# Attention in a two-layer hybrid trunk: probabilities times values as full-width rounded products instead of 64-column fp32 tiles

## The chip, the core and the metric

The kernel runs on one core of a Trainium2 chip. The metric is the device time of one execution in microseconds (us); lower is better. TensorE (PE) does the matrix products and the transposes and writes them to PSUM; VectorE (DVE) and ScalarE (ACT) take them from there; GpSimd (POOL) has a few small powers; SyncE (SP) issues the DMAs.

## The reference, cut to what matters

A backbone of two layers works on 256 latent tokens and 256 context tokens of width 1024. Each layer mixes tokens by four parallel branches, A (a convolution module), B (windowed attention), C (retention) and D (global attention), merges them by gates, and ends with a feed-forward part. Layer 0 carries both kinds of tokens, layer 1 only the latent ones as queries (its keys and values still come from all 512). B and D have 8 query heads and 2 key heads of 64 columns. The place of the change is the last line of

```python
def attend(q, k, v, mask, sink):
    s = jnp.einsum('bhgqd,bhkd->bhgqk', q, k).astype(jnp.float32) * (HEAD_DIM ** -0.5)
    ...
    p = jax.nn.softmax(s, axis=-1)
    ...
    return jnp.einsum('bhgqk,bhkd->bhgqd', p.astype(v.dtype), v)
```

## The kernel before

All large products are done as three products of rounded operands (type fp32r): rounded part times rounded part, and each rounded part times the other's remainder. Weights come by DMA in pieces of 128x1024 (raw), are rounded on ScalarE (wh) and have their remainder taken on VectorE (wl), two halves of 512 columns each. Transposes and some small products are plain fp32.

The order of instructions on every engine is written by a planner within the program. `Model` keeps an estimated clock for each engine, `Engine.us` books each instruction's cost, and `Flow` places side work between the products of the main stream. The main stream (layer, `tm_group`, `proj_a`, `proj_c`, `merge`, `project`, the feed-forward part) issues three products at a time (`mm3`) and then calls `flow.poll()`. Side work stands in generators, which yield what their next step reads; a poll advances those whose data are there by the planner's clocks, in a fixed priority, with at most so many generators of a stream at a time and only while VectorE and ScalarE are not too far ahead of TensorE:

```python
    STREAMS = (("chain2", 3.0, 1), ("pv", 3.0, 1), ("main", 1.5, 2), ("aux", 1.5, 1), ("fill", 0.3, 1))
```

(name, limit in us, generators at a time; each stream is gone over twice in a poll.) The weights' splitting stands ahead of these streams with a limit of 3.0. `flow.until` and `flow.drain` poll without main products until something is done. A wait in the planner's time only orders the instructions; on the chip each engine runs its instructions in that order as soon as their operands are there.

Attention of one branch: `k_gen` and `q_gen` (stream aux) prepare keys and queries; `score_gen` (stream main) makes scores of two heads for one query tile, their exponentials and the normalised probabilities P; when both query tiles of a head pair c are there, it adds a `pv_gen` to stream pv. A `pv_gen` goes over its key blocks kc, four for latent queries (s = 0) and two for context queries (s = 1): four transposes of P into a PSUM bank (ptp), a copy to SBUF (PT), and two products with the values, one head each, that fill the upper and the lower 64 partitions of the bank pv:

```python
                pe.matmul(
                    pv[64 * i:64 * i + 64, 0:256],
                    st["kv"][kt // 2][:, 256 * (kt % 2) + off:256 * (kt % 2) + off + 64],
                    PT[kc][:, 256 * i:256 * i + 256], start=(kc == 0), stop=(kc == nk - 1),
                )
```

Each such fp32 product leaves two records in the trace, so one key block leaves four. At the end pv is rounded (yh) and its remainder taken (yl), which are operands of the merge products mb. There are eight `pv_gen` per branch in layer 0 and four in layer 1. A `score_gen` begins only while fewer than two generators stand in stream pv.

Order of the stages in layer 0: keys and queries of B, branch A's projections and D's queries (tm) with B's attention beside them; then `flow.drain("aux", "main", "pv")`; `merge(stB)` with D's attention beside it; the same drain again; `merge(stD)`; projections of C; `merge(stA)`; `merge(stC)`. Layer 1: A's projections, keys, queries and C's projections with B's attention; `merge(stB)`, whose first product mb waits until B is done, with D's attention beside it; `merge(stD)`, whose first mb waits until D is done; then C and A. The convolution of branch A (tiles co, zp) is on VectorE in the stream fill, the last in priority; it is needed before `merge(stA)`.

Of the kernel before, what the change touches and what calls it, by code (L numbers as in the profile page):

```python
# [21 lines left out]
# columns of the packed per-feature vectors (one layer)  # L22
V_NORM, V_ADAB, V_ADW, V_ADB, V_ALG, V_ALB, V_FDW, V_FDB, V_END = 0, 32, 80, 204, 208, 212, 216, 348, 392
# columns of the packed rows (one layer)
# [3 lines left out]
# groups of adaLN columns: worked out during the last merge, and in the gaps after the two projections  # L28
IN_MERGE = ((4, 5, 6, 7, 8, 9), (7, 8, 9))
IDLE = (((10, 11), (4, 5, 6)), ((10, 11), ()))  # L30
NT = 60      # [128, 512] work tiles
NRAW = 5     # weight pieces on the way in
SIDE = 8     # banks in use when the side work may take one more
NW = 5       # weight pieces as rounded part and remainder


class Model:
    """Estimated clocks of the engines: orders the instructions, decides nothing else."""
# [52 lines left out]
class Engine:  # L91
    """Passes instructions on and books them with the model."""
# [4 lines left out]
    def us(self, op, out, ins, kw):  # L97
        n = _size(out)
        if self.n == "PE":
            if op == "transpose":  # L100
                return 0.123
            if ins[0].dtype == F32R:
                return max(n, 256) / 2400 + 0.002
            if _size(ins[0]) <= 64:
                return 0.25
            return max(4 * n / 2400, 0.235)
        if self.n == "DMA":
            return max(0.1, 1.43e-3 * n)
        n = max([n] + [_size(x) for x in ins])
        psum = any(x.space == bass.MemoryType.PSUM for x in [out, *ins])  # L110
        if self.n == "ACT":
            aps = sum(1 for k in ("scale", "bias") if k in kw and hasattr(kw[k], "shape"))
            return n * 0.833e-3 + (0.05 if psum else 0.093) + 0.093 * aps + (0.06 if "accum_out" in kw else 0)
        if self.n == "POOL":
            return 0.1 + 0.14 * n
        if op == "reciprocal":
            return 0.06 + 8e-3 * n
        aps = 0.06 if any(hasattr(kw.get(k), "shape") for k in ("scalar", "scalar1", "scalar2")) else 0
        if op in ("tensor_scalar", "tensor_copy", "memset") and not psum:
            return 0.06 + 0.52e-3 * n + aps  # L120
        return 0.065 + 1.04e-3 * n + aps
# [21 lines left out]
class Flow:  # L143
    """Places the work of the other engines between the matrix products of the main stream.

    post: generators that follow a product; weights: splitting of the coming weights; streams: generators of the
    branches, in the order of their priority. A generator yields what its next step reads, and is advanced once that
    is there by the model's clocks and the engines are not too far behind.
    """
# [34 lines left out]
    def soon(self, s, slack):  # L184
        """Whether the stream's next step is only short of something that comes shortly."""
        return any(self.there(g, slack) and self.wait.get(g) for g in list(self.q[s])[:1])
# [55 lines left out]
def trunk_kernel(  # L242
# [38 lines left out]
    def turn(t, tag, bufs):  # L281
        """Tells the model whose place a tile takes."""
# [9 lines left out]
    def tmps(count, name, width, dt=F32):  # L292
        """count tiles [128, width]; two share a work tile when the width allows."""
# [14 lines left out]
    CAP = {"m": 4, "s": 4, "t": 2, "v": 1}     # banks of one kind at most  # L308
# [20 lines left out]
    # ---------------------------------------------------------------- constants  # L329
# [5 lines left out]
    xs, xs2 = [[], []], [[], []]      # by feature, and the tiles of two features  # L335
# [23 lines left out]
    hh, hl = [None] * KD, [None] * KD      # normalised input of the sub-layer, rounded and remainder  # L359
# [5 lines left out]
    # ---------------------------------------------------------------- small tables of the layers  # L365
# [9 lines left out]
    def layer_tables(l):  # L375
        row = lambda off, n: row_sb[:, l, off:off + n]
        lt, dec = lts[l], row(R_DEC, 8)
        # log of the decays: min(x, 0) - ln(1 + exp(-|x|))
# [38 lines left out]
    # silu of the two conditioning rows, as a zero padded stationary operand  # L417
# [4 lines left out]
    # ---------------------------------------------------------------- helpers  # L422
# [19 lines left out]
    def chunks(ps_w, rh, rl, cs, nk, c0=0, pre=None):  # L442
        """Products of several weight chunks [nk * 128, 128] with the same features; feature index outermost."""
# [11 lines left out]
    def half(s):  # L455
        return slice(256 * s, 256 * s + 256)
# [4 lines left out]
    # ---------------------------------------------------------------- weights  # L461
# [79 lines left out]
    # ---------------------------------------------------------------- adaLN  # L541
# [8 lines left out]
    def ada_load_half(l, j, h):  # L550
        """Half of a group; a tile holds the columns of two features each."""
# [12 lines left out]
    def ada_gen(l, j, raw, nxt=False, h=None):  # L564
        """A group of columns for both rows; four partial sums, then features on the partitions."""
# [45 lines left out]
    # ---------------------------------------------------------------- RMS norm over features  # L611
    def norm_row(S):
        """S [128, 256]: squares summed over chunks; the row 1/rms on every partition (PSUM)."""
# [7 lines left out]
    def rms_row(b):  # L621
        """From the sums of squares in columns 256:258 to the row in columns 0:256."""
# [54 lines left out]
    def residual(which, s, ys, b, Sx=None, sums=None):  # L677
        """x += gate * rms_norm(y); adds up the squares of the new x over the chunks, in Sx or, on the idle tensor
        engine, per token in the bank sums (one open group: only its first product clears the bank)."""
# [42 lines left out]
    def norm_chain(l, which, s, ys, S):  # L722
        """From the squares of a sub-layer's output to the normalised input of the next sub-layer."""
# [21 lines left out]
    # ---------------------------------------------------------------- heads of B and D  # L745
# [3 lines left out]
    def rope(dst, tmp2, src, cc, ss, lead):  # L749
        """dst = src * cc + swapped halves of src * ss; all views end in 64 head columns."""  # L750
# [7 lines left out]
    def k_gen(l, br, st):  # L758
        """Key heads of all 512 tokens; leaves [kh; kh] and [kl; kl] transposed in st['KT'][2 * head + part]."""
# [3 lines left out]
        st["KT"] = [tmp("KT", F32R) for _ in range(4)]  # L763
        kds = []
        for p in range(2):
# [28 lines left out]
            for t in range(2):  # L794
# [6 lines left out]
                yield  # L801
        for tt, kd in enumerate(kds):
# [14 lines left out]
    def q_gen(l, br, st, tts):  # L817
        """Eight query heads of some token tiles; leaves [qh; ql] transposed in st['QT'][tile, head // 4]."""
# [53 lines left out]
    # ---------------------------------------------------------------- softmax attention  # L872
    def pv_gen(br, st, s, c, P):
        g = c // 2
        nk = 4 if s == 0 else 2
        off = 128 + 64 * g
# [3 lines left out]
        def prod(kc):  # L880
            kt = kc + (0 if s == 0 else 2)
            for i in range(2):
                pe.matmul(
                    pv[64 * i:64 * i + 64, 0:256],
                    st["kv"][kt // 2][:, 256 * (kt % 2) + off:256 * (kt % 2) + off + 64],
                    PT[kc][:, 256 * i:256 * i + 256], start=(kc == 0), stop=(kc == nk - 1),
                )

        for kc in range(nk):
            yield (avail("t"), *(P[q, i] for q in range(2) for i in range(2)))  # L890
            pt = bank("t", "ptp")
            for i in range(2):
                for q in range(2):
                    a = (2 * i + q) * 128
                    pe.transpose(pt[:, a:a + 128], P[q, i][:, kc * 128:kc * 128 + 128], ident)
            if kc:
                if pv is None:
                    yield (avail("v"), PT[kc - 1])
                    pv = bank("v", "pv")
                else:  # L900
                    yield (PT[kc - 1],)
                prod(kc - 1)
            yield (pt,)
            PT[kc] = tmp("PT")
            act.copy(PT[kc], pt)
            free(pt)
        P.clear()
        yield (PT[nk - 1],)
        prod(nk - 1)
        yield (pv,)  # L910
        yh, yl = st["yh"][c][:, half(s)], st["yl"][c][:, half(s)]
        high(pv[:, 0:256], yh)
        yield (yh,)
        low(pv[:, 0:256], yh, yl)
        free(pv)
        st["left"] -= 1
        if not st["left"]:
            st["QT"].clear()
            del st["KT"]
            st["done"] = True  # L920

    def attention(br, st, segs):
        """The score steps of all head pairs and query tiles, in order."""
# [75 lines left out]
    # ---------------------------------------------------------------- one layer  # L999
    def layer(l, segs):  # L1000
# [58 lines left out]
        # ---- branch A: gated input, depthwise convolution, norm over channels  # L1059
# [119 lines left out]
        # ---- branch C: bidirectional retention, one head at a time  # L1179
# [132 lines left out]
        # ---- gated merge of one branch  # L1312
# [41 lines left out]
        # ---- output projections  # L1354
        def project(which, rh, rl, nk, ys, first, last):
            """ys (+)= products; in the last group the tail serves the latent tokens first, and the norms follow."""
# [23 lines left out]
            def final_feature(m):  # L1380
                """The last output, scaled by its gain and with the tokens on the partitions; its squares."""
# [55 lines left out]
            if last:  # L1437
                # several outputs at a time while the last of the features are still on their way
# [24 lines left out]
        def x_tokens():  # L1463
            """The latent stream with the tokens on the partitions, for the last addition."""
# [11 lines left out]
        # ---- ConvFFN  # L1476
# [74 lines left out]
        # ================================================================ order of work  # L1551
# [99 lines left out]
    # ================================================================ program  # L1651
    def start_chain(s):
        """The first normalised input; the squares of two features at a time."""
# [49 lines left out]
def _layout(inp):  # L1703
# [52 lines left out]
    def units(w, n):  # L1756
        """[..., K, C] -> [..., C / n, 128, K / 128, n]"""
# [43 lines left out]
```

## Time and profile before

| | us |
|---|---|
| median of 3 runs | 1671.38 |
| lowest and highest of them | 1669.04, 1671.46 |
| span of the profiled execution | 1670.4 |

The profile gives the span of its execution, from the first to the last instruction; that execution's own device time is not listed beside it, and the median of the runs is 1.0 us above the span. All instructions that pass through the planner bear line 127, so groups are told apart by their tiles (out<-in). A busy TensorE is not TensorE at its peak: records of products overlap, so the cost of one is read from the distance of starts. The granted clock is full but for short stretches (mean 0.984).

### The profile page before, as it was taken

The page shows a single profiled execution, that of the slowest core. Times are in us where ns is not written, and L with a number is a line of the kernel's source. Part 1 is how long each engine was busy: PE and PEld are TensorE (multiplying, and loading weights), DVE is VectorE, ACT ScalarE, POOL GpSimd, SP SyncE. Part 2 cuts the span into 40 slices and gives each one's busy share as a digit, 9 for nine tenths or more (in the row PEclk, how much of TensorE's full clock was granted, in tenths as well). Part 3 has the DMA queues.
Part 4 walks back from the last instruction along what each step waited for, and adds up shares of the span by engine and source line. Part 5 has one row for each costly group of instructions (what it writes and reads, how often), then busy time and mean ns, then how long its engine had stood idle before and what let it go on. Part 6 is the DMA issues. An engine that isn't in the chain of part 4 may idle for free.

```text
span 1670.4 us, 25191 instructions
## 1 busy us (share of the span) xinstructions
PE 1631.0 (98%) x9578; PEld 1353.8 (81%) x9578; DVE 1142.2 (68%) x2406; ACT 793.8 (48%) x1706; POOL 35.9 (2%) x38
## 2 busy tenths in 40 slices
PE   6999999999999999999999999899999999999998
PEld 3776776788777678778888888788688989899997
DVE  4666898994584434766356556799887866578876
ACT  3666466324322334444344334456666444556653
POOL 0000000000010000000000000000100000000000
PEclk9999999999999999899999999899999999989999
DMA  9421211223314756153323327144143375726552
GB/s 339 148 64 38 76 64 51 76 89 107 102 63 154 270 207 238 38 191 101 101 88 101 101 73 254 52 147 144 40 131 114 117 266 188 251 89 216 183 173 73
DMA packets 82121, 222.20 MB, mean 133 GB/s; under 512 B 8912, under 2 KB 17616, under 8 KB 82000
## 3 DMA queue, kind: packets, MB, share of 16 engines
q1 hardware_dynamic: 81712, 220.07, 39.7%
q8 instruction: 75, 1.23, 0.3%
q10 hardware_dynamic: 288, 0.52, 0.1%
q14 instruction: 46, 0.38, 0.1%
HBM read 219.51 MB, written 1.05 MB: 132 GB/s over the span
## 4 chain that ended last, share of the span: by engine, by line
PE 82%; issue 12%; DMA 2%; DVE 2%; ACT 1%; SPq 0%; POOL 0%; POOLq 0%; DVEq 0%; ACTq 0%
PE mg L127 16%; PE op L127 11%; PE tm L127 11%; PE mb L127 8%; PE fa L127 7%; PE fb L127 7%; PE pv L127 3%; PE sc L127 2%; PE cqk L127 2%; PE adp L127 2%; PE pa L127 2%; PE ptp L127 2%; PE pg L127 2%; PE f L127 1%; DMA adw<-in_ada_w 1%
## 5 line engine op out<-in xcount | busy, mean ns | idle before, releaser
L127 DVE TENSOR_TENSOR wl<-raw,wh 128x512 fp32r<-128x512 f32 (+1 forms) x624 | 404.3, 678 | 206.5 <-ACT wh L127 201.7
L127 ACT CAST wh<-raw 128x512 fp32r<-128x512 f32 (+1 forms) x624 | 358.0, 613 | 178.6 <-PE fb L127 47.6
L127 PE MATMUL mg<-hh,wh 128*128 128x512 f32 (+1 forms) x512 | 180.5, 353 | 0.0
L127 PE MATMUL mg<-hl,wh 128*128 128x512 f32 (+1 forms) x512 | 172.4, 337 | 0.0
L127 PE MATMUL mg<-hh,wl 128*128 128x512 f32 (+1 forms) x512 | 172.4, 337 | 0.0
L127 DVE SCALAR_TENSOR_TENSOR co<-zp,hdw,co 128x482 f32<-128x482 f32 (+29 forms) x240 | 129.1, 599 | 0.0
L127 PE MATMUL op<-gh,wh 128*128 128x256 f32 (+1 forms) x370 | 122.2, 330 | 0.0
L127 PE MATMUL op<-gl,wh 128*128 128x256 f32 (+1 forms) x370 | 121.5, 328 | 0.0
L127 PE MATMUL op<-gh,wl 128*128 128x256 f32 (+1 forms) x370 | 121.5, 328 | 0.0
L127 PEld LDWEIGHTS mg<-hh,wh 128*128 128x128 f32 x512 | 97.1, 190 | 26.6 <-issue 15.6
L127 ACT ACTIVATE mth<-mg 128x512 f32<-128x512 f32 (+1 forms) x64 | 31.4, 491 | 179.9 <-PE mg L127 179.4
L127 PE MATMUL tm<-wh,hh 128*128 128x512 f32 x272 | 112.3, 413 | 2.8 <-ACT hh L127 2.8
L127 PE MATMUL tm<-wh,hl 128*128 128x512 f32 x272 | 107.1, 394 | 2.5 <-DVE hl L127 2.5
L127 PE MATMUL fa<-hh,wh 128*128 128x512 f32 (+1 forms) x320 | 108.1, 338 | 0.0
L127 PE MATMUL fa<-hl,wh 128*128 128x512 f32 (+1 forms) x320 | 107.6, 336 | 0.0
L127 PE MATMUL fb<-hh,wh 128*128 128x512 f32 (+1 forms) x320 | 107.6, 336 | 0.0
L127 PE MATMUL fa<-hh,wl 128*128 128x512 f32 (+1 forms) x320 | 107.6, 336 | 0.0
L127 PE MATMUL fb<-hh,wl 128*128 128x512 f32 (+1 forms) x320 | 107.6, 336 | 0.0
L127 PE MATMUL fb<-hl,wh 128*128 128x512 f32 (+1 forms) x320 | 107.6, 336 | 0.0
L127 PE MATMUL tm<-wl,hh 128*128 128x512 f32 x272 | 106.9, 393 | 0.0
L127 PEld LDWEIGHTS mg<-hh,wl 128*128 128x128 f32 x512 | 97.1, 190 | 10.4
L127 PEld LDWEIGHTS mg<-hl,wh 128*128 128x128 f32 x512 | 97.3, 190 | 7.7
(250 smaller groups left out, 3588.9 us busy)
## 6 DMA issues: line engine op xcount, KB each, us to landing
adw<-in_ada_w SPq DMA_DIRECT2D x192, 256.0 KB, 5.7
raw<-in_w_fm SPq DMA_DIRECT2D x88, 512.0 KB, 3.5
raw<-in_f_up SPq DMA_DIRECT2D x88, 512.0 KB, 3.6
raw<-in_w_tm SPq DMA_DIRECT2D x40, 512.0 KB, 3.6
raw<-in_w_br SPq DMA_DIRECT2D x32, 512.0 KB, 3.5
raw<-in_f_d SPq DMA_DIRECT2D x32, 512.0 KB, 3.5
raw<-in_w_o SPq DMA_DIRECT2D x16, 512.0 KB, 3.7
raw<-in_f_d SPq DMA_DIRECT2D x16, 384.0 KB, 3.0
```

Source lines behind the costliest of these rows:

```text
L127: r = f(*a, **kw)
```

## The change

The products become rounded ones of full width. `k_gen` writes the values' rounded part and, beside it, their remainder into 128 stationary columns (VV). The copy of the transposes becomes a rounding (PTh), and a remainder (PTl) is taken on VectorE from the same bank. Each key block is two products of 128x128 with 512 columns, one with PTh and one with PTl, all into one group of the bank pv: its upper 64 partitions hold the sum with the values' rounded part, the lower 64 that with their remainder, for both heads beside each other. On the way out two copies on ScalarE move halves across partitions, and two sums on VectorE add them; then rounding and remainder as before, from SBUF. A step's products are issued after the rounding of the next block's transposes. The planner's cost of a rounded product is changed too. The remaining lines of the diff take away comments.

```diff
@@ class Engine: us
             if ins[0].dtype == F32R:
-                return max(n, 256) / 2400 + 0.002
+                return max((n + 32) / 2400, 0.107)
...
@@ def k_gen
         st["KT"] = [tmp("KT", F32R) for _ in range(4)]
+        st["VV"] = [tmp("VV", F32R).rearrange("p (t h a d) -> p t h a d", t=2, h=2, a=2) for _ in range(2)]
+        vs = [kv[p].rearrange("p (t c) -> p t c", t=2)[:, :, 128:256].rearrange("p t (h d) -> p t h d", h=2)
+              for p in range(2)]
+        for p in range(2):
+            act.copy(st["VV"][p][:, :, :, 0, :], vs[p])
...
+        for p in range(2):
+            vv = st["VV"][p]
+            dve.tensor_tensor(out=vv[:, :, :, 1, :], in0=vs[p], in1=vv[:, :, :, 0, :].bitcast(F32), op=ALU.subtract)
         for tt, kd in enumerate(kds):
...
@@ def pv_gen
         g = c // 2
         nk = 4 if s == 0 else 2
-        off = 128 + 64 * g
...
         def prod(kc):
             kt = kc + (0 if s == 0 else 2)
+            vv = st["VV"][kt // 2][:, kt % 2, g].rearrange("p a d -> p (a d)")
             for i in range(2):
-                pe.matmul(
-                    pv[64 * i:64 * i + 64, 0:256],
-                    st["kv"][kt // 2][:, 256 * (kt % 2) + off:256 * (kt % 2) + off + 64],
-                    PT[kc][:, 256 * i:256 * i + 256], start=(kc == 0), stop=(kc == nk - 1),
-                )
+                pe.matmul(pv, vv, PT[kc][i], start=(kc == 0 and i == 0), stop=(kc == nk - 1 and i == 1))
...
+            yield (pt,)
+            PT[kc] = [tmp("PTh", F32R), tmp("PTl", F32R)]
+            act.copy(PT[kc][0], pt)
+            yield (PT[kc][0],)
+            low(pt, PT[kc][0], PT[kc][1])
+            free(pt)
             if kc:
                 if pv is None:
-                    yield (avail("v"), PT[kc - 1])
+                    yield (avail("v"), *PT[kc - 1])
                     pv = bank("v", "pv")
-                else:
-                    yield (PT[kc - 1],)
                 prod(kc - 1)
-            yield (pt,)
-            PT[kc] = tmp("PT")
-            act.copy(PT[kc], pt)
-            free(pt)
+                del PT[kc - 1]
         P.clear()
-        yield (PT[nk - 1],)
+        yield tuple(PT[nk - 1])
         prod(nk - 1)
         yield (pv,)
+        t = tmp("pvt")
+        act.copy(t[0:64, 0:256], pv[64:128, 0:256])
+        act.copy(t[64:128, 0:256], pv[0:64, 256:512])
+        yield (t,)
+        y = t[:, 256:512]
+        dve.tensor_tensor(out=y[0:64], in0=pv[0:64, 0:256], in1=t[0:64, 0:256], op=ALU.add)
+        dve.tensor_tensor(out=y[64:128], in0=pv[64:128, 256:512], in1=t[64:128, 0:256], op=ALU.add)
+        free(pv)
         yh, yl = st["yh"][c][:, half(s)], st["yl"][c][:, half(s)]
-        high(pv[:, 0:256], yh)
+        yield (y,)
+        high(y, yh)
         yield (yh,)
-        low(pv[:, 0:256], yh, yl)
-        free(pv)
+        low(y, yh, yl)
```

## Rows read from the trace of the kernel before

**Rows 1.** The page's first part: busy time, share of the span, instructions.
```profile
PE 1631.0 (98%) x9578; PEld 1353.8 (81%) x9578; DVE 1142.2 (68%) x2406; ACT 793.8 (48%) x1706; POOL 35.9 (2%) x38
```

**Rows 2.** The page's chain that ended last, shares of the span by engine.
```profile
PE 82%; issue 12%; DMA 2%; DVE 2%; ACT 1%; SPq 0%; POOL 0%; POOLq 0%; DVEq 0%; ACTq 0%
```

**Rows 3.** The chain in order of time, its long pieces: start, length, what.
```profile
802.24 43.52 PE op L127 x192
...
1423.96 23.05 PE op L127 x192
```

**Rows 4.** Groups by form: busy us, mean ns of one | idle before, releaser.
```profile
L127 PE MATMUL pv<-PT,kv 128*64 128x256 f32 x320 | 52.2, 405 | 0.0
...
L127 DVE TENSOR_TENSOR wl<-raw,wh 128x512 fp32r<-128x512 f32 x592 | 387.4, 685 | 200.6 <-ACT wh L127 195.9 <-DMA adw<-in_ada_w 4.0
...
L127 DVE TENSOR_TENSOR yl<-pv,yh 128x256 fp32r<-128x256 f32 x24 | 10.1, 422 | 16.7 <-ACT yh L127 16.4
...
L127 ACT CAST yh<-pv 128x256 fp32r<-128x256 f32 x24 | 9.0, 373 | 33.7 <-PE pv L127 33.6
```

**Rows 5.** Timeline of PE around one pv step: start, length, what.
```profile
119.58 0.40 PE L127 MATMUL pg<-hh,wl 128*128 128x512 f32 x1
119.90 0.65 PE L127 MATMUL pv<-PT,kv 128*64 128x256 f32 x4
120.48 0.50 PE L127 MATMUL pg<-hh,wh 128*128 128x512 f32 x1
120.82 0.39 PE L127 MATMUL pg<-hl,wh 128*128 128x512 f32 x1
```

**Rows 6.** Tiles ptp and pv by branch: ns min/median/max, first and last start.
```profile
L127 DVE TENSOR_TENSOR yl<-pv,yh x8: 415/424/426, 121.0 to 184.3; 128x256 fp32r<-128x256 f32 x8
...
L127 PE MATMUL ptp<-cst_sb,P x96: 270/272/273, 233.0 to 300.9; 128*128 128x128 f32 x96
...
L127 DVE TENSOR_TENSOR yl<-pv,yh x8: 414/423/426, 242.8 to 305.0; 128x256 fp32r<-128x256 f32 x8
...
L127 DVE TENSOR_TENSOR yl<-pv,yh x4: 416/423/425, 1182.4 to 1219.4; 128x256 fp32r<-128x256 f32 x4
...
L127 DVE TENSOR_TENSOR yl<-pv,yh x4: 416/420/425, 1255.4 to 1288.3; 128x256 fp32r<-128x256 f32 x4
```

**Rows 7.** Timeline: first product of the four merges of B and D.
```profile
194.84 0.39 PE L127 MATMUL mg<-hh,wh 128*128 128x512 f32 x1
...
304.52 0.50 PE L127 MATMUL mg<-hh,wh 128*128 128x512 f32 x1
...
1230.12 0.28 PE L127 MATMUL mg<-hh,wh 128*128 128x256 f32 x1
...
1290.36 0.28 PE L127 MATMUL mg<-hh,wh 128*128 128x256 f32 x1
```

**Rows 8.** Timeline of one two-step generator of branch D, layer 0.
```profile
287.55 0.60 PE L127 MATMUL ptp<-cst_sb,P 128*128 128x128 f32 x4
...
288.19 0.59 ACT L127 COPY PT<-ptp 128x512 f32<-128x512 f32 x1
...
292.34 0.65 PE L127 MATMUL pv<-PT,kv 128*64 128x256 f32 x4
...
293.04 0.37 ACT L127 CAST yh<-pv 128x256 fp32r<-128x256 f32 x1 [1.73 <-PE pv L127]
...
293.45 0.42 DVE L127 TENSOR_TENSOR yl<-pv,yh 128x256 fp32r<-128x256 f32 x1 [1.21 <-ACT yh L127]
...
293.72 0.60 PE L127 MATMUL ptp<-cst_sb,P 128*128 128x128 f32 x4
```

**Rows 9.** Windows: stretch, length, then busy us (instructions) of PE, PEld, DVE, ACT.
```profile
100.00:305.00 205.00, 205.00 (x1099) 147.84 (x1098) 160.77 (x365) 125.56 (x324) 9.51 (x6) 1.00 0.17 56
305.00:440.00 135.00, 135.00 (x613) 112.08 (x612) 93.44 (x151) 46.01 (x82) 1.39 (x1) 1.00 0.31 99
1100.00:1345.00 245.00, 244.83 (x1540) 202.69 (x1539) 212.44 (x503) 145.45 (x341) 9.03 (x9) 1.00 0.36 116
```

More of the change, by code (lines that the diff above doesn't have):

```diff
@@ L918, in pv_gen @@
             st["QT"].clear()
-            del st["KT"]
+            del st["KT"], st["VV"]
             st["done"] = True
```

## The prediction, made before the changed kernel was run

> **What bounds the kernel now.** The page's first part comes first: TensorE is busy 98% of a span of 1670.4 us, VectorE 68%, ScalarE 48% [rows 1]. The chain of waits agrees: 82% of it is TensorE's products, 12% is issue, and DMA and VectorE have 2% each [rows 2]. So a microsecond taken from TensorE's stream is a microsecond of the span, as long as nothing else becomes late. How fast that stream runs is read from long pieces of the chain without side work: 192 rounded products of 512 columns in 43.52 us, 0.2267 us each, and 192 of 256 columns in 23.05 us, 0.120 us each [rows 3].
>
> The change touches only the step "probabilities x values" (tile pv), so next come its groups and its place in time. A pv step (one key block of one head pair) leaves four records, and there are 320 / 4 = 80 steps [rows 4]. Around one such step the timeline shows the third pg product at 119.58, the step at 119.90, the next pg products at 120.48 and 120.82 [rows 5]. From 119.58 to 120.82 are 1.24 us; the two pg products in it would take 0.453, so a step costs 0.787 us: 0.58 for itself, 0.10 before it and 0.11 behind it.
>
> The second question is what else has a deadline. The pv stream lets only one generator advance at a time, so the 24 generators (four or two steps each; eight per branch in layer 0, four in layer 1) are one chain per branch. In layer 0, branch D's chain runs from 233.0 to 305.4 [rows 6], and the main stream, which must drain it before the next merge, begins that merge at 304.52 [rows 7]: the chain's last step is issued and the next product follows at once, without slack. Branch B's chain ends at 184.7 and the drain is at 194.84: 10 us of slack. In layer 1 the chains end at 1219.8 and 1288.7; they are needed 24 products of 0.12 us after 1230.12 and 1290.36, at 1233.0 and 1293.2 [rows 6, 7].
>
> **TensorE's side.** The new step is two rounded products of 512 columns: 0.453 us. If the gaps around a step go with the fp32 tiles, it saves 0.787 - 0.453 = 0.333 us, in all 80 x 0.333 = 26.7 us; if they stay, 0.58 - 0.453 = 0.13 us, 10 us in all. I take the first, since rounded products of one form follow each other without such gaps in [rows 5]: 8.0 us per branch in layer 0 (24 steps), 5.3 in layer 1 (16 steps).
>
> Here a rule of the Trainium skill speaks against the change (TensorEngine Tiling (Array Packing), Theoretical Speedup): a stationary operand of at most 64 columns lets two tiles work side by side, up to twice the rate, and the change gives that up. The row agrees that they overlap, four records of 0.405 us in 0.65 us [rows 4, 5]. By the rule alone the kernel would lose the 30 us of rival (e) below; by the 0.2267 us of [rows 3] it wins the 26.7 above. The same page of the Trainium skill (Key Properties) has a change of tiling mode drain TensorE, and the 0.10 and 0.11 us around a step agree with that.
>
> **VectorE's and ScalarE's side.** Each step adds a remainder of 128x512, like the weights' (685 ns); each generator adds two sums on 64 partitions x 256, bounded above by the 128x256 remainder (422 ns) and below by nothing; each branch and layer two remainders of the values (422 ns) [rows 4]. VectorE: 80 x 0.685 + 48 x 0.422 + 8 x 0.422 = 78.5 us, of which 48 fall in layer 0. ScalarE: two copies a generator and two roundings a branch and layer at about 373 ns, 56 x 0.373 = 21 us; the copy of the transposes (0.59 us [rows 8]) becomes a rounding of the same size. Is there cover? In layer 0 VectorE is busy 160.8 of 205 us while attention runs and 93.4 of 135 us behind it [rows 9]: 44 + 42 us idle. What yields is branch A's convolution, which has the lowest priority and is not needed before merge A, far behind. So 48 us are hidden there. In layer 1 it is busy 212.4 of 245 us, and 30.4 more leave 2 us: tight. I charge 2 us to the retention behind it (bounds 0 and 10).
>
> **The chain's side.** After its last step a generator now goes step, rounding, remainder, and the next generator's transposes follow: 292.34, 293.04, 293.45, 293.72 [rows 8]. The change puts in: a remainder before the last step (0.69), two copies (0.75) and two sums (0.84) behind it, 2.28 us of work in series. It takes out 0.333 us for each step, 1.0 us for three (the mean of four and two). So a generator becomes at least 1.3 us longer. Three hand-overs are added as well, and a step is only issued at a poll, every three products, 0.68 us: at most 2.0 us, and on the mean half of it. I take 1.3 + 1.0 = 2.3 us, bounds 1.3 and 3.3.
>
> Now the deadlines. When the main stream has run out, the rest of the chain runs without products between its steps. A two-step generator took 6.2 us (287.55 to 293.72 [rows 8]), 8.5 with the change; its work alone, transposes 0.60, copy 0.59, remainder 0.69, step 0.65, copies 0.75, sums 0.84, rounding 0.37 and remainder 0.42, is 4.9, and a pair of convolution pieces between (1.4) makes 6.3. So the rest runs in about 0.72 of its time.
> Layer 0, B: chain to 184.7 + 8 x 2.3 = 203.1; main stream out at 194.8 - 8.0 = 186.8; 16.3 x 0.72 = 11.7; end 198.5, later by 3.7.
> Layer 0, D: relative to its start, chain to 323.9, main stream out at 296.5; 27.4 x 0.72 = 19.7; end 316.2 for 304.5, later by 11.7.
> Layer 1, B: chain to 1229.0, needed at 1227.7; earlier by 4.0. D: chain to 1288.7 - 4.0 + 9.2 = 1293.9, needed at 1293.2 - 9.3 = 1283.9; 10 x 0.72 = 7.2; 1291.1, earlier by 2. With the 2 us charged above, layer 1 gives nothing.
> At 1.3 us a generator the same sums give +4 in layer 0 and -6 in layer 1, at 3.3 us +27 and about +3.
>
> **The planner's cost line.** A rounded product is now booked as (n + 32) / 2400: 0.2267 and 0.120 us, which is what [rows 3] show, for 0.215 and 0.109 before. Times of execution do not depend on it, only the order of all engines. TensorE idles 39.4 us in the whole span [rows 1], which bounds a gain; a loss has no row. I take nothing, bounds 5 us either way.
>
> **Sum.** 1670.4 + 3.7 + 11.7 + 0 = 1685.8 us of span. The profile gives a span only; the median of the runs shown is 1.0 us above it, so about 1687 us.
>
> **The rivals.** (a) Forecast: attention's chain ends both drains of layer 0, 1687 us, own range 1676 to 1698. Chance 0.40.
> (b) TensorE's saving comes through: 1671.4 - 26.7 = 1645 us if the chain is nowhere late. The point that decides is about 1.3 us a generator, where the sums above cancel; at 0.3 us they give -8 in layer 0 and -9 in layer 1, some 1655 us. For it: the order is made anew, and in layer 1 chains had slack; against it: no slack in [rows 7]. Range 1645 to 1662. Chance 0.36.
> (c) VectorE becomes the bound: in branch D's stage of layer 0 and in layer 1 half of the 78.5 us is not covered, weights' remainders come late, and some 25 us are added to the forecast: 1712 us. For it: 2 us of room in layer 1; against it: the convolution yields. Chance 0.10.
> (d) The two sides cancel: 1668 to 1675 us. Chance 0.12.
> (e) Full width loses the overlap of the two tiles, so that a step takes twice its 0.58 us: 80 x (1.16 - 0.787) = 30 us more, 1702 us. Against it stand the 0.2267 us of [rows 3]. This is the Trainium skill's rule weighed above. Chance 0.02.
>
> **How the numbers follow.** About 0.2% (3.3 us) can be told from no change here. Slower: (a), (c), (e), 0.52; same: (d), 0.12; faster: (b), 0.36. The range 1648 to 1708 leaves out the top of (c) and the bottom of (b), less than 2 in 10.
>
> **What would show it.** Right: pv products 0.227 us apart without gaps around them; generators some 2 us longer; TensorE idle for 10 to 20 us before the merges at 199 and 316 us, its waits ending with ScalarE's or VectorE's parts of pv; no idle time in layer 1. Wrong: no gap in TensorE's stream at those two places (b), or weights' remainders that TensorE waits for (c).

## The result, and the profile after

The changed kernel takes 1721.48 us (median of 4 runs, 1720.95 to 1722.84) beside 1670.21 us of the kernel before on the same chip: a ratio of 1.0302, interval 1.029 to 1.0314. It is slower by 51 us, where some 16 were forecast, and above the range. Its span is 1721.0 us, so the 50.6 us are all in the span.

The page's first part and chain of the changed kernel, which answer to [rows 1, 2]:

```profile
PE 1635.2 (95%) x9418; PEld 1379.1 (80%) x9418; DVE 1208.1 (70%) x2533; ACT 821.6 (48%) x1771; POOL 36.4 (2%) x38
...
PE 62%; DVE 18%; issue 13%; ACT 4%; DMA 2%; POOL 0%; SPq 0%; DVEq 0%; POOLq 0%; ACTq 0%
PE mg L127 11%; PE op L127 11%; PE tm L127 7%; PE fa L127 6%; PE fb L127 6%; PE mb L127 6%; DVE co L127 4%; DVE wl L127 3%; PE adp L127 2%; DVE PTl L127 2%; PE pg L127 2%; PE pa L127 2%; PE cqk L127 1%; DVE nm L127 1%; PE f L127 1%
```

The reader is to see that VectorE's share of the chain that ends last rose from 2% to 18%, and TensorE's fell from 82% to 62%, although VectorE is busy only 66 us more (78.5 were forecast). Something now waits for VectorE in places; an average over the span does not say where. The largest of VectorE's groups on the chain is the convolution, co, with 4%.

The products themselves did what was forecast. PE's timeline of the changed kernel around two steps, the counterpart of [rows 5]:

```profile
117.44 0.40 PE L127 MATMUL pg<-hh,wl 128*128 128x512 f32 x1
117.68 0.40 PE L127 MATMUL pv<-PTh,VV 128*128 128x512 f32 x1
117.91 0.39 PE L127 MATMUL pv<-PTl,VV 128*128 128x512 f32 x1
118.14 0.39 PE L127 MATMUL pg<-hh,wh 128*128 128x512 f32 x1
118.37 0.40 PE L127 MATMUL pg<-hl,wh 128*128 128x512 f32 x1
```

Every start is 0.23 us behind the last: a step takes 0.46 us and has no gap around it, where it took 0.787 before. The side-by-side tiles that were given up are not missed; the rule of the Trainium skill weighed in the prediction (TensorEngine Tiling (Array Packing), Theoretical Speedup) does not decide here.

Most of the time is lost at the two drains of layer 0. PE's timeline of the changed kernel at the end of the first and at the second, the counterpart of [rows 7] (starts; in brackets the idle time before and what ended it):

```profile
207.94 0.63 PE L127 MATMUL mg<-hh,wh 128*128 128x512 f32 x1
...
301.96 0.40 PE L127 MATMUL mb<-yh,wl 128*128 128x512 f32 x1
302.19 0.40 PE L127 MATMUL pv<-PTh,VV 128*128 128x512 f32 x1
303.35 0.50 PE L127 MATMUL pv<-PTl,VV 128*128 128x512 f32 x1 [0.77 <-DVE PTl L127]
...
345.59 0.80 PE L127 MATMUL pv<-PTl,VV 128*128 128x512 f32 x1 [2.10 <-DVE PTl L127]
...
347.04 0.63 PE L127 MATMUL mg<-hh,wh 128*128 128x512 f32 x1
347.46 0.63 PE L127 MATMUL mg<-hl,wh 128*128 128x512 f32 x1
```

The merge of B has its last product at 301.96 and the merge of D its first at 347.04: for 45 us TensorE has attention's own work only. The first drain, between D's queries and the merge of B, lasts from 182.9 to 207.9 in the same way. The first products of these merges are at 194.84 and 304.52 in [rows 7], at 207.94 and 347.04 now: the stretch up to the first became 13.1 us longer, the one between them 139.1 - 109.7 = 29.4 us. That is 42.5 of the 50.6 us. The other 8 are the balance of gains and losses behind layer 0's attention: layer 0's last merge begins 46.2 us late (575.91 for 529.73), the merge of B in layer 1 only 36.5 (1266.62 for 1230.12), with part of B's attention still to come, and the end of the span 50.6. TensorE idles again in two waits behind that merge; their windows (stretch, length, busy us of PE, PEld, DVE, ACT, POOL, then the granted clock):

```profile
1269.00:1282.00 13.00, 9.76 (x47) 7.24 (x46) 11.70 (x24) 7.50 (x18) 0.00 (x0) 0.87 0.39 122
...
1337.00:1346.00 9.00, 5.30 (x26) 3.04 (x26) 8.79 (x20) 3.71 (x8) 0.00 (x0) 1.00 0.78 247
```

What each engine does in the two waits of layer 0 is in the same windows:

```profile
183.00:208.00 25.00, 14.19 (x51) 9.21 (x50) 22.53 (x50) 12.39 (x35) 0.00 (x0) 0.64 0.12 42
...
302.00:347.00 45.00, 26.08 (x86) 18.62 (x85) 43.74 (x90) 18.89 (x54) 0.00 (x0) 0.62 0.07 23
```

VectorE is nearly full, 22.5 of 25 and 43.7 of 45 us. With the convolution's tile co alone, the same windows:

```profile
183.00:208.00 25.00, 0.00 (x0) 0.00 (x0) 9.38 (x14) 0.00 (x0) 0.64 0.12 42
...
302.00:347.00 45.00, 0.00 (x0) 0.00 (x0) 21.71 (x32) 0.00 (x0) 0.62 0.07 23
```

Almost half of VectorE's time in the second wait is the convolution, the work of lowest priority, which nothing needs before merge A at 483. VectorE's timeline there shows how it stands in the way:

```profile
331.57 1.39 DVE L127 SCALAR_TENSOR_TENSOR co<-zp,hdw,co 128x504 f32<-128x504 f32 x2
332.88 0.85 DVE L127 TENSOR_TENSOR pvt<-pv,pvt 64x256 f32<-64x256 f32 x2
333.77 1.40 DVE L127 SCALAR_TENSOR_TENSOR co<-zp,hdw,co 128x506 f32<-128x506 f32 x2
335.09 0.42 DVE L127 TENSOR_TENSOR yl<-pvt,yh 128x256 fp32r<-128x256 f32 x1
335.42 1.40 DVE L127 SCALAR_TENSOR_TENSOR co<-zp,hdw,co 128x508 f32<-128x508 f32 x2
336.85 0.69 DVE L127 TENSOR_REDUCE nm<-sc 128x2 f32<-128x512 f32 x1
337.58 0.17 DVE L127 TENSOR_SCALAR nb<-nm 128x2 f32<-128x2 f32 x1
337.65 1.28 DVE L127 TENSOR_TENSOR PTl<-ptp,PTh 128x512 fp32r<-128x512 f32 x2
```

Between the links of the chain (pvt, yl, PTl) stands a pair of convolution pieces, 1.4 us for the two, each time. In the second wait PE's idle time has two causes in the list of waits (engine, what it waited for: us in total, times, longest):

```profile
PE pv L127 <- DVE PTl L127: 14.6, 9, 3.2
PE pv L127 <- ACT PTh L127: 4.3, 3, 2.1
```

The chains are longer everywhere. Tiles ptp and pvt of the changed kernel in branch D's stage of layer 0, for [rows 6]:

```profile
L127 PE MATMUL ptp<-cst_sb,P x96: 270/273/421, 246.3 to 341.3; 128*128 128x128 f32 x96
...
L127 DVE TENSOR_TENSOR yl<-pvt,yh x8: 417/418/421, 266.1 to 350.3; 128x256 fp32r<-128x256 f32 x8
```

From 246.3 to 350.7 are 104.4 us for eight generators, 13.1 each; before it was 72.4, 9.1 each.

### The profile page after: what moved, and what is told of

It reads as the page before. It is cut to its first block, busy times and chain, and to the rows that moved or that the text cites. A ratio compares the mean times of both kernels' runs of the same rounds, so it can differ in the third digit from the quotient of the medians.

```text
span 1721.0 us, 25110 instructions
## 1 busy us (share of the span) xinstructions
PE 1635.2 (95%) x9418; PEld 1379.1 (80%) x9418; DVE 1208.1 (70%) x2533; ACT 821.6 (48%) x1771; POOL 36.4 (2%) x38
## 4 chain that ended last, share of the span: by engine, by line
PE 62%; DVE 18%; issue 13%; ACT 4%; DMA 2%; POOL 0%; SPq 0%; DVEq 0%; POOLq 0%; ACTq 0%
PE mg L127 11%; PE op L127 11%; PE tm L127 7%; PE fa L127 6%; PE fb L127 6%; PE mb L127 6%; DVE co L127 4%; DVE wl L127 3%; PE adp L127 2%; DVE PTl L127 2%; PE pg L127 2%; PE pa L127 2%; PE cqk L127 1%; DVE nm L127 1%; PE f L127 1%
```

## The experiments

A hand-over is the step from one engine's result to the next engine's work on it. Theory 1: the generators of stream pv are one serial chain; the change makes each longer, and in the waits the convolution's pieces and the planner's hand-overs stand between its links. Theory 2: the planner's new cost line makes the order anew and brings the loss. Theory 3: VectorE's total load is the bound. Each ratio is to the kernel before on the same chip; 1.0302 is that of the change.

**Only the cost line.** The kernel before with
```diff
-                return max(n, 256) / 2400 + 0.002
+                return max((n + 32) / 2400, 0.107)
```


> The kernel before with nothing but the new cost line of the planner. Theory 1 (the serial chain of pv generators is longer, and VectorE's convolution pieces stand in front of its steps where TensorE waits): the cost line is no cause, 1665 to 1676 us. Theory 2 (the cost line makes the order anew and brings much of the loss): 1685 to 1721 us. Theory 3 (VectorE's total load is the bound): no added load here, 1665 to 1676 us.

1672.15 us, 1.001 (1.0 to 1.0019). Theory 2 falls for the kernel before.

**The change with the old cost line.** The same edit undone in the changed kernel.

> The changed kernel with the old cost line. Theory 1: the loss stays, 1710 to 1732 us, with TensorE idle before the merges of B and D in layer 0. Theory 2: most of the loss goes, 1670 to 1700 us. Theory 3: as theory 1.

1738.35 us, 1.041 (1.0389 to 1.043). Theory 2 falls here too, with the opposite sign: the new line takes 17 us off the change's loss. No theory had foreseen that, and the 1710 to 1732 us of theory 1 were missed. The two waits of this kernel, in its windows:

```profile
177.20:214.70 37.50, 20.69 (x73) 14.16 (x73) 34.00 (x77) 17.35 (x52) 0.00 (x0) 0.58 0.04 14
304.90:355.70 50.80, 30.55 (x105) 21.35 (x104) 46.26 (x95) 21.83 (x61) 0.00 (x0) 0.61 0.07 21
```

They are 12 and 6 us longer than with the new line.

**Control.** To hold back the convolution needs two more work tiles, so one weight buffer is given up:
```diff
-NT = 60
-NRAW = 5
+NT = 62
+NRAW = 4
```


> Control for the next one: the changed kernel with one weight buffer less and two work tiles more. All theories: 1716 to 1727 us.

1722.28 us, 1.0311 (1.0293 to 1.033): as the change.

**The convolution held in the waits.** The control with
```diff
-    def poll(self):
+    def poll(self, idle=False):
...
         for s, lim, width in self.STREAMS:
+            if s == "fill" and idle and self.q["pv"]:
+                continue
...
     def until(self, cond):
...
-            if self.poll():
+            if self.poll(idle=True):
```


> The changed kernel (buffers as in the control) in which the convolution is not advanced while the main stream waits and attention's generators are unfinished. Theory 1: VectorE's convolution pieces (9.5 of 25 us and 21 of 45 us in the two waits of layer 0) no longer stand in front of the chain, the waits become 8 and 18 us shorter or more, and the time 1690 to 1705 us. Theory 3: the convolution's work only moves and is waited for later, 1716 to 1727 us. Theory 2: 1716 to 1727 us.

1708.41 us, 1.0229 (1.021 to 1.0248): 14 us less than the control, against theory 3, but less than theory 1 had it. Windows of this kernel in its two waits:

```profile
182.00:202.00 20.00, 12.45 (x51) 8.48 (x49) 16.01 (x39) 13.12 (x37) 0.00 (x0) 0.74 0.18 52
299.00:332.00 33.00, 22.12 (x92) 15.21 (x91) 24.55 (x60) 20.02 (x57) 0.00 (x0) 0.79 0.10 32
```

The waits shrank from 25 to 20 and from 45 to 33 us, and VectorE is no longer full in them (16.0 of 20, 24.6 of 33). The convolution has 2.8 and 0.9 us left in them; what remains is the chain with almost no such work in its way.

**Two generators at a time.** The changed kernel with
```diff
-    STREAMS = (("chain2", 3.0, 1), ("pv", 3.0, 1), ...
+    STREAMS = (("chain2", 3.0, 1), ("pv", 3.0, 2), ...
...
-    CAP = {"m": 4, "s": 4, "t": 2, "v": 1}
+    CAP = {"m": 4, "s": 4, "t": 2, "v": 2}
```


> The changed kernel with two generators of stream pv advanced at a time and two banks for pv. Theory 1 (the generators are one serial chain, and its longer links make TensorE wait): the chains overlap, the waits before the merges of B and D in layer 0 shrink, 1690 to 1710 us. Theory 3 (VectorE's total load is the bound): 1715 to 1727 us.

1689.68 us, 1.0115 (1.0097 to 1.0132). With the same load, letting two generators overlap is worth 32 us. Its second wait, in its windows:

```profile
292.00:317.00 25.00, 15.74 (x55) 10.86 (x53) 23.28 (x52) 14.43 (x41) 0.00 (x0) 0.66 0.12 42
```

The first wait is down to 3 us; the second is 25 us, with VectorE nearly full again.

**Without the probabilities' remainders.** The changed kernel with
```diff
-            PT[kc] = [tmp("PTh", F32R), tmp("PTl", F32R)]
+            PT[kc] = [tmp("PTh", F32R)]
...
-            low(pt, PT[kc][0], PT[kc][1])
...
-            for i in range(2):
-                pe.matmul(pv, vv, PT[kc][i], start=(kc == 0 and i == 0), stop=(kc == nk - 1 and i == 1))
+            pe.matmul(pv, vv, PT[kc][0], start=(kc == 0), stop=(kc == nk - 1))
```


> The changed kernel without the remainders of the probabilities: PTl and its 80 products are left out of the computation. It takes 55 us of work from VectorE, 18 us of products from TensorE, and one link from each chain. Theory 1: the tail with its copies and sums stays in the chain, so only part of the loss goes beyond the 18 us of products: 1680 to 1700 us. Theory 3: with the load nearly all of the loss goes, 1645 to 1670 us.

1681.83 us, 1.0065 (1.005 to 1.008): 40 us less than the change, where 80 products, 18 us of TensorE's time, are left out as well. With 46 of the 65.9 us that the change added gone from VectorE's busy time, the kernel is still slower than before, as theory 1 has it.

**Without the tail.** The control with the copies and sums left out:
```diff
-        t = tmp("pvt")
-        act.copy(t[0:64, 0:256], pv[64:128, 0:256])
...
-        high(y, yh)
+        high(pv[:, 0:256], yh)
         yield (yh,)
-        low(y, yh, yl)
+        low(pv[:, 0:256], yh, yl)
+        free(pv)
```


> The changed kernel (buffers as in the control) that rounds the first half of pv as it comes out: the two copies and two sums of the halves are left out of the computation. It takes 20 us from VectorE, 18 us from ScalarE and three hand-overs from the end of each generator. Theory 1: each generator loses some 2.6 us or more, the two waits of layer 0 become some 15 us shorter each, 1685 to 1705 us. Theory 3: in proportion to VectorE's work (20 of 78 us), 1705 to 1715 us.

1692.45 us, 1.0132 (1.0117 to 1.0147): 30 us less than the control. The tail is a quarter of the work that was forecast for VectorE and brings more than its share in proportion.

**Load without a longer chain.** The kernel before with
```diff
             act.copy(PT[kc], pt)
             free(pt)
+            dve.tensor_tensor(out=tmp("PTx"), in0=PT[kc], in1=PT[kc], op=ALU.subtract)
```


> The kernel before with a remainder-sized operation on VectorE after each copy of transposes, whose result nothing reads: 80 x 0.685 = 55 us of VectorE's work without a longer chain. Theory 1: 1668 to 1682 us. Theory 3: most of the loss is there, 1695 to 1715 us.

1688.3 us, 1.0109 (1.0092 to 1.0126): between the theories. 55 us on VectorE that nothing reads cost 18 us, so theory 1 in its pure form is wrong as well: load alone opens the drains, here by 5 us before the merge of B and 12 before that of D. Windows of this kernel in the two, and what TensorE waits for in the first:

```profile
192.50:197.60 5.10, 2.11 (x14) 0.91 (x13) 1.28 (x2) 4.48 (x12) 0.00 (x0) 1.00 0.00 0
301.50:314.10 12.60, 8.67 (x50) 4.83 (x49) 11.24 (x28) 8.38 (x24) 0.00 (x0) 0.86 0.26 84
...
PE pv L127 <- ACT PT L127: 3.0, 2, 2.0
```

VectorE is busy 11.2 us of the second, but only 1.3 of the first, where TensorE waits for ScalarE's copies PT. So the first is not due to a full VectorE; how the added load brings it about, through the planner's order perhaps, is not shown.

**Links without load.** The kernel before with operations of 2 columns:
```diff
             act.copy(PT[kc], pt)
+            yield (PT[kc],)
+            x = small(2, "lk")
+            dve.tensor_tensor(out=x, in0=PT[kc][:, 0:2], in1=PT[kc][:, 2:4], op=ALU.subtract)
             free(pt)
...
         yield (pv,)
+        x = small(2, "lk")
+        act.copy(x, pv[:, 0:2])
+        yield (x,)
+        x2 = small(2, "lk")
+        dve.tensor_tensor(out=x2, in0=pv[:, 0:2], in1=x, op=ALU.add)
+        yield (x2,)
```


> The kernel before with as many links more in each generator as the change has, but of 2 columns: a small operation on VectorE between the copy of the transposes and the release of their bank, and two small ones, on ScalarE and VectorE, before the last rounding. No load to speak of is added. Theory 1 (hand-overs of the serial chain cost by themselves): the waits before the merges of layer 0 open, 1680 to 1700 us. Theory 3: 1668 to 1676 us.

1695.94 us, 1.015 (1.0135 to 1.0166): 25 us for hand-overs with hardly any work in them (0.15 us for each link on VectorE). Its wait before the merge of D, in its windows, and the convolution's part of them:

```profile
296.00:322.00 26.00, 17.30 (x99) 10.30 (x98) 25.36 (x65) 14.11 (x42) 0.00 (x0) 0.83 0.12 41
...
296.00:322.00 26.00, 0.00 (x0) 0.00 (x0) 15.73 (x23) 0.00 (x0) 0.83 0.12 41
```

VectorE is full here too, 15.7 us of it with the convolution: so in this wait the links' own price and that of queueing behind the convolution are not told apart. The links' own price is to be read in branch B's first four generators, where TensorE has main products all the time and the convolution begins only at 156 us with the links and in the change. Tile yl there, in the kernel before, in this one and in the changed one:

```profile
L127 DVE TENSOR_TENSOR yl<-pv,yh x4: 423/424/426, 121.0 to 159.7; 128x256 fp32r<-128x256 f32 x4
...
L127 DVE TENSOR_TENSOR yl<-pv,yh x4: 415/417/426, 123.8 to 172.7; 128x256 fp32r<-128x256 f32 x4
...
L127 DVE TENSOR_TENSOR yl<-pvt,yh x4: 418/424/427, 120.5 to 173.0; 128x256 fp32r<-128x256 f32 x4
```

From one yl to the next are 12.9, 16.3 and 17.5 us: six links of 2 columns add 3.4 us to a generator of four steps, 0.57 us each; the change adds 4.6.

**Links and load together.** The kernel before with the links above, the first of them as large as a remainder (`in0=PT[kc], in1=PT[kc]` into a work tile).

> The kernel before with both additions of the two earlier runs: a remainder-sized operation on VectorE for each key block that is now a link of the chain, and two small links at a generator's end; products stay fp32. If links (25 us) and load (18 us) add: 1708 to 1720 us, so that the changed kernel, at 1721, got nothing from its cheaper products. If they overlap: 1690 to 1705 us.

1693.03 us, 1.0134 (1.0116 to 1.0151): they do not add. That a link which waits for a full VectorE is one delay and not two would explain it, but is not shown.

**The products alone.** The kernel before with the values' two parts (VV), rounded transposes (the rounded part is multiplied twice, so that the products are as many as in the change; remainders, copies and sums are left out), and
```diff
-                pe.matmul(
-                    pv[64 * i:64 * i + 64, 0:256],
-                    st["kv"][kt // 2][:, 256 * (kt % 2) + off:256 * (kt % 2) + off + 64],
-                    PT[kc][:, 256 * i:256 * i + 256], start=(kc == 0), stop=(kc == nk - 1),
-                )
+                pe.matmul(pv, vv, PT[kc], start=(kc == 0 and i == 0), stop=(kc == nk - 1 and i == 1))
...
-            PT[kc] = tmp("PT")
+            PT[kc] = tmp("PT", F32R)
```


> The kernel before with the full-width rounded products and the values' parts alone: the probabilities' remainder is left out (the rounded part is multiplied twice), and so are the copies and sums of the halves. TensorE's term of 26.7 us by itself, with the chain as before: 1640 to 1650 us. If only the 10 us without the gaps around a step come: 1656 to 1664 us. If cheaper products give nothing because the chain is the bound: 1665 to 1675 us.

1650.38 us, 0.9884 (0.9868 to 0.9901): 20 us faster. A part of the rest of the 26.7 is given back at the drain before the merge of D, for here, too, the chain ends last; PE's timeline of this kernel:

```profile
186.73 0.39 PE L127 MATMUL mg<-hh,wh 128*128 128x512 f32 x1
...
284.51 0.40 PE L127 MATMUL mb<-yh,wl 128*128 128x512 f32 x1
...
289.05 0.98 PE L127 MATMUL ptp<-cst_sb,P 128*128 128x128 f32 x7 [1.18 <-DVE P L127]
291.08 1.21 PE L127 MATMUL pv<-PT,VV 128*128 128x512 f32 x4 [1.05 <-ACT PT L127]
292.13 0.40 PE L127 MATMUL mg<-hh,wh 128*128 128x512 f32 x1
```

Between the first products of the merges of B and D are 105.4 us, 4.3 less than before, where 24 steps save 8.0: 3.7 us are given back there. The other 3 were not traced.

**Versions that should win.** The change with both remedies (two generators at a time, convolution held, buffers as in the control):

> The changed kernel with two generators of stream pv at a time and the convolution held while the main stream waits for attention (buffers as in the control). If serial chain and convolution ahead of it are two causes that add, their gains (32 and 14 us) add as far as waits are left: 1672 to 1682 us. If both act on the same waiting time, no more than the first alone: 1685 to 1692 us.

1681.65 us, 1.0067 (1.005 to 1.0085): the gains add in part, and the kernel is still slower than before.

The kernel before with two generators at a time:

> The kernel before with two generators of stream pv at a time. Theory 1 (TensorE is the bound there and no wait is open): 1664 to 1674 us. If attention's serial chain was already a bound before the change: 1650 to 1662 us.

1665.78 us, 0.9972 (0.9961 to 0.9983): 5 us faster than the kernel before, with the computation unchanged.

The change without the probabilities' remainders, with both remedies:

> The changed kernel without the remainders of the probabilities (PTl and its 80 products are left out of the computation), with two generators of stream pv at a time and the convolution held in the waits. Theory 1: with the chain's length and VectorE's work mostly gone, TensorE's saving of 27 us and 18 us of products left out come through in part: 1640 to 1662 us. Theory 3: 1665 to 1682 us.

1657.26 us, 0.9918 (0.9901 to 0.9934). It beats both kernels, at the price of probabilities in rounded form only.

## Why the prediction was wrong

**TensorE's side: right.** 0.333 us a step were forecast; the trace has 0.787 - 0.46 = 0.33. Alone it is worth 20 us of the 26.7; 3.7 of the difference are lost at the drain of branch D, which had no slack, as the prediction read from [rows 7].

**The place of the loss: right.** TensorE idles before the two merges of layer 0 that the prediction named. Layer 1, from which nothing was forecast, gives a little loss: 9.7 us are gained from layer 0's last merge to the first of layer 1, 14.1 are lost behind it, and TensorE idles 7 us in two waits there, where no idle time was forecast.

**The chain's side: the term that was mis-sized.** 2.3 us a generator and 0.72 of that pace in the waits gave +3.7 and +11.7 us at the two drains; they became 13.1 and 29.4. With the drains' own end the two chains of layer 0 were forecast at 89 and 83 us; they last 104.3 (107.3 to 211.6) and 104.4. How much each part brings is read from four kernels: products alone 1650, with the tail (no remainders) 1682, with the remainders (no tail) 1692, both 1721. So the tail costs some 30 us and the remainders some 40, in either order; 1650 + 31 + 42 = 1723. Three limits go with this sum: the kernel without remainders has one product a step less, 18 us in all, so that its tail may cost up to as much more; the one without tail has the control's buffers; and the one with products alone is built on the kernel before and so has its order and cost line. That the sum comes out is therefore in part luck. The prediction had charged links and work with about 42 us in all (26.7 won, 15.4 lost on balance); by the products alone they cost 1721 - 1650 = 71.

**Why it was mis-sized.** Two steps failed. First, the prediction charged a generator with three hand-overs of half a poll, 0.34 us, and with one remainder. But the edit puts a wait for PTh into every key block, and frees the bank of the transposes only behind the remainder, besides the hand-overs at the end; and a link of 2 columns costs 0.57 us in a stage in which TensorE always has main products. So a generator of four steps became 4.6 us longer there, above the upper bound of 3.3 for a mean generator.

Second, "What yields is branch A's convolution" is not so in the waits. The convolution yields to the other streams at the moment when the planner picks work; once issued, its 1.4 us pair stands in VectorE's queue ahead of the next link. It took 21.7 of 45 us, held back it gave 14 us. The forecast had one such pair in a two-step generator and 6.3 us for it in the waits. Tile yl of the last four such generators in the changed kernel and with the convolution held (the first of the five is the end of the generator before):

```profile
L127 DVE TENSOR_TENSOR yl<-pvt,yh x5: 417/418/421, 314.1 to 350.3; 128x256 fp32r<-128x256 f32 x5
...
L127 DVE TENSOR_TENSOR yl<-pvt,yh x5: 424/426/428, 310.2 to 334.1; 128x256 fp32r<-128x256 f32 x5
```

They take 9.1 us each with the convolution in the way, with three or four pairs in one, and 6.0 without it. The two waits shrink by 17 us when it is held back and the time by 14: its work has to be done elsewhere.

The idle TensorE also lost its clock: the granted clock is 0.62 in the second wait, so part of it ran at 1.2 GHz instead of 2.4, and the merge's first products start 0.42 us apart instead of 0.23. What this cost by itself no run separates.

**VectorE's load: counted as hidden, and not.** The 48 us in layer 0 had cover on paper, by [rows 9]. A load that nothing reads, 55 us in both layers, cost 18 us by itself. It does not come on top of the links: both together cost 23, no more than the links alone. Cover was there in the sum over the stage; but with this load alone VectorE was nearly full in the wait before the merge of D. In that before the merge of B it was not, and the cause there stays open.

**The planner's cost line: right to leave it out, wrong that 5 us bound it.** On the kernel before it changes next to nothing; with the change it is a help of 17 us. With the old line the waits of layer 0 are 12 and 6 us longer, and the merge of D begins 8.6 us later (355.66 for 347.04); why the order that it makes is worse stays open.

**The rivals.** (b) is what the products alone show, 1650 us, and the tail and remainders take away. Its point of decision, 1.3 us a generator, was passed by far: 4.0 us in branch D's stage, waits included. (c), 1712 us by a full VectorE, is the nearest in time, and its picture, VectorE full in branch D's stage, is in the windows; but its mechanism is not the one that the runs show: TensorE waits there for PTl and PTh and not for the weights' remainders, with the same load two generators at a time gain 32 us, and links without load lose 25. (e) is refuted by the 0.23 us between the products.

## What to carry to other kernels

Before adding links to a chain that a busy engine waits for, look at who ends last at the next drain: at the drain of branch D chain and TensorE ended together, so what was added to the chain was lost there, and of 8.0 us saved on TensorE 3.7 were given back. A hand-over of a serial chain has a price of its own, here 0.57 us with hardly any work in it; where operations must be added to it, let two chains run at a time first, which gained 32 us in the changed kernel and 5 us in the one before. Work of low priority covers nothing if, once issued, it stands in the queue ahead of a link: hold it back while something waits.

## What was not expected of the hardware

Two 64-column fp32 tiles side by side cost 0.787 us with the gaps around them, 1.7 times the 0.46 us of two full-width rounded products of 512 columns each. In the two waits, where TensorE had attention's pieces with pauses between them, the mean granted clock was 0.64 and 0.62, so it stood at its lower level for a good part of either.
